# Hymba layer in float32: a scheduler that knows the shared port and measured steps, and small matmuls in runs of one array form

## Chip, cores and metric

One core of one Trainium2 chip. The metric is the device time of one launch in microseconds. PE is TensorE, PEld its weight loads, DVE is VectorE, ACT is ScalarE, POOL is GpSimd, SP is SyncE, which issues the DMAs. "Us" stands for microseconds throughout.

## The reference

One layer for 1024 prompt tokens and 8 samples of 4 tokens (1056 columns in all), in float32, model width 1024:

```python
def layer_forward(x, lw, rel_table, kv_cache, ssm_h0):
    h = rmsnorm(x, lw['norm_mix'])
    proj = h @ lw['w_in']                                    # 1024 -> q 512 | k 128 | v 128 | u 512
    q, k, v, u = jnp.split(proj, ...)                        # 8 query heads, 2 key heads of 64
    o_attn = band_attention(...)                             # blocks of 128 queries, window 128, bias, sinks
    o_ssm, h_last = s5_mixer(u, ssm_h0, ...)                 # 32 groups of 16 channels, state 64, then half-GLU
    merged = jnp.concatenate([rmsnorm(o_attn, ...), rmsnorm(o_ssm, ...)], axis=-1)
    x = x + merged @ lw['w_out']
    hm = rmsnorm(x, lw['norm_mlp'])
    x = x + jnp.square(jax.nn.relu(hm @ lw['w_up'])) @ lw['w_down']   # 1024 -> 4096 -> 1024
    return x, new_k, new_v, jnp.real(h_last), jnp.imag(h_last)
# afterwards: rmsnorm with norm_final
def s5_mixer(u, h0, ...):
    lam_bar = jnp.exp(lam * step)
    bu = jnp.einsum('blgc,gpc->blgp', u, b_bar)              # + lam_bar * h0 at the first token
    _, h = lax.associative_scan(combine, (a, bu), axis=1)    # h[t] = lam_bar h[t-1] + bu[t]
    y = jnp.real(jnp.einsum('blgp,gcp->blgc', h, c)) + d * u
    g = jax.nn.gelu(y)
    return g * jax.nn.sigmoid(g @ w_glu + b_glu), h[:, -1]
```

## The kernel before

Activations lie with channels on the partitions and tokens along the free axis, in rows of 128x1056. A large matmul (called bulk here) multiplies a 128x128 weight tile with a third of a row, 128x352. Each float32 operand is split into a high part, rounded for the fast float32 form of PE, and the rest; three products (high x high, low x high, high x low) accumulate in PSUM. 5760 bulk matmuls make up the in-projection, w_out, w_glu and the MLP. A weight piece of four tiles (`wr`, 256 KB) is split into `wh` (ACT or DVE) and `wl` (DVE or POOL), each with two buffers; `R` are 35 row buffers, `big` larger ones that live long, `PS` the eight PSUM banks. The program runs through: the split of x by rows and the first norm's sums; the in-projection; S5 in four steps s0 to s3 of eight groups each (tables by `F`, `K`; `X = F^T U` and its scan; `YT`); attention for the samples and for eight blocks b0 to b7; w_out; GELU and GLU; the SSM norm; the MLP; the last norm.

Small matmuls stand in between. `X` and `use` have 128 rows and 64 columns, in two column halves. In `att_block` a score matmul multiplies 64 rows (one key head, a half of the array's rows) by 128 columns, out 128x256: four query heads x three products for one key head, then a masked copy by DVE in PSUM, then the same for the other head in the other buffer of two banks (`pq2`). `PV` has 128 rows and 64 columns, out 64x512, one key head in each column half. The samples' PV has for each sample and head a matmul of 128 rows and one of 4 rows.

Nothing is issued in the order of the text. Every call is recorded as an `Op` (`Plan.record`) with a cost from `op_cost` for each engine that may do it (`ew` operations: DVE or POOL; copies: ACT or DVE). `Plan.schedule` then places one operation after another: of each engine the candidate that can start soonest, and among those with the same start the one with the highest priority, by the longest chain of costs behind it. Small matmuls get 100 on top there:

```python
                if e == "PE":
                    t = a[2][0].tile
                    p = group[t.mate] + (8.0 if t.units else 0.0) + (0.0 if o.bulk else 100.0)
...
                if cand is None or s < cand[0] - 1e-9 or (s <= cand[0] + 1e-9 and (p, -o.i) > cand[1]):
                    cand = (s, (p, -o.i), o, a)
```

`SCRIPT` gives the order of record and `BOOST` numbers for a few parts. `issue` emits the calls in the planned order, all from one line (L339), so groups in the profile are told apart by tiles and shapes. On the chip each engine runs its own list in order and waits for semaphores.

Of the kernel before, what the change touches and what calls it, by code (L numbers as in the profile page):

```python
# [18 lines left out]
# ---------------------------------------------------------------- planning: the kernel is written in program order, its  # L19
# operations are recorded, and a list scheduler puts them in the order in which they are issued  # L20
# [17 lines left out]
class View:  # L38
    """part of a planned tile: the elements it covers, and how the real tile gives it"""
# [33 lines left out]
class Op:  # L73
    __slots__ = ("alts", "tiles", "succ", "ndep", "prio", "avail", "i", "table", "src", "why", "s", "boost", "bulk")


QW = 0.5
# [4 lines left out]
TABLE = {AF.Exp: 1, AF.Tanh: 1, AF.Sin: 2, AF.Sqrt: 3}  # L82


def op_cost(eng, method, args, kw):
    out = args[0]
# [18 lines left out]
    if eng == "DVE":  # L105
# [8 lines left out]
        return (0.13 if psum and method == "scalar_tensor_tensor" else 0.07) + n / 960  # L114
# [4 lines left out]
    bc = len(vs) < 3 or any(a.ix.strides[-1] == 0 for a in vs[1:])  # L119
    return 0.15 + n * (1.66 if bc else 2.1) / 1000  # L120


class Plan:
# [4 lines left out]
    # -- tiles  # L128
# [11 lines left out]
    # -- operations  # L140
# [3 lines left out]
    def record(self, calls):  # L144
        o = Op()
        o.i, o.boost, o.bulk = len(self.ops), self.boost, self.bulk
        o.alts = [(e, m, a, k, op_cost(e, m, a, k)) for e, m, a, k in calls]
        a, k = calls[0][2:]
        views = [(v, True) for v in (a[0], k.get("accum_out")) if isinstance(v, View)]
        views += [(v, False) for v in (*a[1:], *(x for n, x in k.items() if n != "accum_out")) if isinstance(v, View)]  # L150
        o.tiles = list({v.tile: None for v, _ in views})
# [19 lines left out]
        if calls[0][0] == "PE":  # L171
            # accumulation groups of a bank stay in order
            v = a[0]
            key = v.box()[2] // 512
            prev = v.tile.last.get(key)
            if prev is not None and o.i not in prev.succ:
                prev.succ[o.i] = False
                o.ndep += 1
            v.tile.last[key] = o
# [7 lines left out]
    # -- the list scheduler  # L187
    def schedule(self):
# [5 lines left out]
        # a group of matmuls counts as its most urgent one  # L194
# [7 lines left out]
        table = [0]  # L202
        pend = {e: [] for e in ENG}
# [24 lines left out]
        def slot(t):  # L228
            """(time, units) of the best free place, or None"""
# [22 lines left out]
        while len(seq) < len(ops):  # L252
            best = None
            for e, lst in pend.items():
                cand = None
                fe = free[e]
                for o, a in lst:
                    s = max(fe, o.avail)
                    if cand is not None and s > cand[0] + 1e-9:
                        continue  # L260
                    if len(o.alts) > 1:
                        fin = s + a[4]
                        if any(b[0] != e and max(free[b[0]], o.avail) + b[4] + queue(b[0], o) < fin for b in o.alts):
# [38 lines left out]
            else:  # L302
# [4 lines left out]
                end = free[e] = s + c  # L307
            for t in o.tiles:
# [22 lines left out]
    # -- issue  # L331
    def issue(self, engines, make):
        res = lambda x: x.get() if isinstance(x, View) else x
        for n, (s, o, a) in enumerate(self.seq):
# [4 lines left out]
            getattr(engines[e], m)(*[res(x) for x in args], **{k: res(x) for k, x in kw.items()})  # L339
# [25 lines left out]
# rows: which ones a part of the kernel takes  # L365
# [6 lines left out]
# order of record up to the MLP  # L372
# [5 lines left out]
def body(tc, I, O, dbg=None):  # L378
# [6 lines left out]

    def dump(name, ap):
# [6 lines left out]
    def copy(out, in_):  # L393
        """ScalarE or VectorE"""
# [1073 lines left out]
```

## Time and profile before

| | us |
|---|---|
| time, median of 3 runs | 1217.54 |
| lowest, highest | 1208.55, 1219.12 |
| profiled execution, span from first to last instruction | 1209.6 |
| of it up to the start of the MLP (bulk matmul 1440) | 443.5 |
| mean granted clock of PE, share of full speed | 0.966 |

The profiled execution has no time of its own beside the span. The span is near the lowest of the three runs; sums below are made in it. PE's granted clock is a share of 2.4 GHz.

### The profile page before, as it was taken

How to read it: one execution, taken by the hardware profiler on the slowest of the kernel's cores; microseconds unless marked ns; L12 is line 12 of the kernel's file. 1: busy time of each engine (PE TensorE's matmuls, PEld its weight loads, DVE VectorE, ACT ScalarE, POOL GpSimd, SP SyncE). 2: the span in 40 equal slices, each digit the busy share in tenths (PEclk: the TensorE clock that was granted, in tenths of full speed). 3: DMA queues.
4: the chain of work that ended last, by engine and by line, in shares of the span. 5: the costliest groups of instructions: out<-in, count | busy, mean ns of one | idle time of the engine just before them, and what ended most of it. 6: DMA issues, size and time to landing. Idle time of an engine off the chain costs nothing.

```text
span 1209.6 us, 17482 instructions
## 1 busy us (share of the span) xinstructions
PE 1153.0 (95%) x7231; PEld 1109.0 (92%) x7231; DVE 670.9 (55%) x970; ACT 274.2 (23%) x512; POOL 277.0 (23%) x259
## 2 busy tenths in 40 slices
PE   6989999979888999999999999999999999999997
PEld 6888996658778999999999999999999999999996
DVE  8687747898789894522522533432432432534575
ACT  4212134632143321211111111111111111111241
POOL 4066414575463140020010010010011011000011
PEclk9989989969889999999999999999999999999997
DMA  6312320023331111111211111111111211121212
GB/s 234 102 47 71 98 46 11 9 47 93 85 99 44 37 44 43 44 44 44 53 44 45 53 44 36 52 44 44 53 44 45 53 44 44 44 52 44 79 54 92
DMA packets 55711, 69.71 MB, mean 58 GB/s; under 512 B 12184, under 2 KB 31808, under 8 KB 55616
## 3 DMA queue, kind: packets, MB, share of 16 engines
q1 hardware_dynamic: 55632, 68.59, 20.3%
q8 instruction: 57, 0.93, 0.4%
q14 instruction: 22, 0.18, 0.0%
HBM read 58.96 MB, written 6.15 MB: 54 GB/s over the span
## 4 chain that ended last, share of the span: by engine, by line
PE 69%; DVE 3%; ACT 1%; issue 0%; DVEq 0%; ACTq 0%; POOL 0%
PE PS L339 69%; DVE R L339 2%; DVE big L339 1%; ACT P L339 1%; ACT wh L339 0%; ACT R L339 0%; DVE wl L339 0%; DVE rsc L339 0%; DVE wh L339 0%; DVEq L1464 0%; ACT rsc L339 0%; ACTq L339 0%; DVE rs L339 0%; POOL R L339 0%; DVEq L339 0%
## 5 line engine op out<-in xcount | busy, mean ns | idle before, releaser
L339 PE MATMUL PS<-R,wh 128*128 128x352 f32 x3840 | 749.2, 326 | 19.4 <-DVE wh L339 10.1
L339 PEld LDWEIGHTS PS<-R,wh 128*128 128x128 f32 x3840 | 643.2, 191 | 25.6 <-DVE wh L339 10.5
L339 PE MATMUL PS<-R,wl 128*128 128x352 f32 x1920 | 430.1, 326 | 0.9 <-POOL wl L339 0.5
L339 PEld LDWEIGHTS PS<-R,wl 128*128 128x128 f32 x1920 | 331.5, 191 | 4.8 <-issue 2.1
L339 POOL TENSOR_TENSOR wl<-wr,wh 128x512 fp32r<-128x512 f32 x64 | 92.7, 1449 | 700.2 <-ACT wh L339 490.0
L339 ACT ACTIVATE wh<-wr 128x512 fp32r<-128x512 f32 x144 | 91.0, 632 | 649.9 <-PE PS L339 637.4
L339 DVE TENSOR_TENSOR wl<-wr,wh 128x512 fp32r<-128x512 f32 x96 | 70.2, 731 | 255.4 <-ACT wh L339 249.9
L339 DVE TENSOR_TENSOR big<-PS,big 128x1056 f32<-128x1056 f32 (+2 forms) x80 | 82.5, 1035 | 167.0 <-PE PS L339 166.9
L339 PE MATMUL PS<-R,R 128*128 128x384 f32 (+9 forms) x816 | 140.8, 342 | 19.1 <-DVE R L339 8.4
L339 PEld LDWEIGHTS PS<-R,R 128*128 128x128 f32 (+3 forms) x816 | 111.3, 196 | 40.2 <-POOL R L339 15.4
L339 DVE TENSOR_TENSOR R<-R,R 64x508 f32<-64x508 f32 (+8 forms) x55 | 44.6, 823 | 4.9 <-ACT R L339 4.3
L339 POOL TENSOR_TENSOR R<-R,R 128x512 f32<-128x512 f32 (+6 forms) x34 | 39.3, 1163 | 32.6 <-DVE R L339 23.9
L339 DVE TENSOR_TENSOR P<-P 128x1056 f32<-128x1056 f32 x32 | 40.3, 1259 | 6.6 <-ACT P L339 6.6
L339 DVE TENSOR_TENSOR P<-P,R 128x1056 f32<-128x1056 f32 x32 | 40.4, 1263 | 0.9
L339 DVE TENSOR_TENSOR R<-P,R 128x1056 fp32r<-128x1056 f32 x32 | 40.3, 1258 | 1.1
L339 ACT ACTIVATE R<-PS 128x512 f32<-128x512 f32 (+3 forms) x40 | 22.6, 570 | 75.9 <-PE PS L339 70.0
L339 ACT ACTIVATE P<-PS 128x1056 f32<-128x1056 f32 (+2 forms) x35 | 34.6, 988 | 8.8 <-PE PS L339 8.8
L339 ACT ACTIVATE R<-R 128x352 f32<-128x352 f32 (+4 forms) x32 | 25.8, 823 | 38.8 <-DVE R L339 38.5
L339 DVE SCALAR_TENSOR_TENSOR R<-R,R 128x352 f32<-128x352 f32 (+5 forms) x28 | 32.2, 1186 | 1.3 <-ACT R L339 1.3
L339 ACT ACTIVATE R<-R,sx 128x129 f32<-128x129 f32 x68 | 26.5, 392 | 22.7 <-DVE sx L339 22.7
L339 ACT ACTIVATE P<-big 128x384 f32<-128x384 f32 (+2 forms) x29 | 19.1, 662 | 50.5 <-DVE big L339 46.1
L339 POOL TENSOR_TENSOR big<-big,R 128x1056 f32<-128x1056 f32 x7 | 25.8, 3680 | 10.1 <-DVE big L339 9.9
(140 smaller groups left out, 691.1 us busy)
## 6 DMA issues: line engine op xcount, KB each, us to landing
wr<-in_w_up_dram SPq DMA_DIRECT2D x64, 256.0 KB
wr<-in_w_down_dram SPq DMA_DIRECT2D x64, 256.0 KB
R<-in_xT_dram SPq DMA_DIRECT2D x15, 528.0 KB
wr<-in_w_in_dram SPq DMA_DIRECT2D x20, 256.0 KB
wr<-in_w_out_dram SPq DMA_DIRECT2D x16, 256.0 KB
out_y_dram<-big SPq DMA_DIRECT2D x8, 384.0 KB
R<-R SPq DMA_DIRECT2D x32, 68.0 KB
R<-R SPq DMA_DIRECT2D x32, 64.0 KB
```

The lines of the kernel that those rows point to most:

```text
L339: getattr(engines[e], m)(*[res(x) for x in args], **{k: res(x) for k, x in kw.items()})
```

## The change

Five edits in the planner and in how small matmuls are recorded; `SCRIPT`, `BOOST` and the arithmetic stay, and comments are stripped.

- `op_cost` has other numbers for PE, DVE (operands with a stride of eight elements or more count 1.87 times) and POOL.
- `port` tells which DVE and POOL operations use the port that both share; such an operation isn't planned to start while one on the other engine is planned to run (`held`).
- `SWITCH`: a matmul whose array form (rows and columns of its weight tile, in classes 32, 64, 128) differs from that of the one before it is planned 0.2 later.
- `Run` records a group of small matmuls as one operation that nothing can come between: sums and rows of the norms, K, X, use, YT, transposes in fours, sample scores, PV.
- In `att_block` one run of 24 score matmuls alternates between the two key heads, into four banks at once (`pq4`); the four PV matmuls are a run; the samples' PV is done in two passes, all 128-row matmuls first and then all 4-row ones. A `start` flag then stands on the first matmul of a pass alone.

```diff
@@ op_cost
         if args[1].dt == F32R:
-            return 0.0025 + max(n, 256) / 2400
+            return max(0.056, 0.0133 + n / 2400)
         if m <= 64:
-            return max(0.06, 0.03 + n / 1200)
-        return max(0.134, 0.0025 + n / 600)
+            return max(0.107, n / 600)
+        return max(0.224, 0.013 + n / 600)
...
-        return (0.13 if psum and method == "scalar_tensor_tensor" else 0.07) + n / 960
+        slow = 1.87 if any(far(a) for a in vs) else 1.0
+        return (0.13 if psum and method == "scalar_tensor_tensor" else 0.07) + n / 960 * slow
...
-    bc = len(vs) < 3 or any(a.ix.strides[-1] == 0 for a in vs[1:])
-    return 0.15 + n * (1.66 if bc else 2.1) / 1000
+    return 0.16 + n * 1.75 / 1000
...
+def port(eng, method, args):
+    if method == "memset" or eng not in ("DVE", "POOL"):
+        return False
+    if eng == "POOL":
+        return True
+    big = [a for a in args[1:] if isinstance(a, View) and a.ix.size > a.ix.shape[0]]
+    sb = [a for a in big if a.tile.space != "PS"]
+    if method in ("tensor_scalar", "tensor_copy"):
+        return len(sb) == len(big) and args[0].tile.space != "PS"
+    return len(sb) > 1 or method == "tensor_tensor_scan"
@@ schedule
                     s = max(fe, o.avail)
+                    if e in o.port:
+                        s = max(s, held[other[e]])
+                    if e == "PE" and o.form != shape[0]:
+                        s += SWITCH
@@ class Run
+    def __exit__(self, *_):
+        c = self.calls
+        cost = sum(op_cost("PE", m, a, k) for m, a, k in c) / self.side
+        self.plan.record([("PE", *c[0])], c, cost)
@@ rs_sum
-            for b in blocks:
-                n = min(128, NT - b * 128)
-                c = (b - b0) * 128
-                pe.matmul(p[0:n, b - p0:b - p0 + 1], ss[:, c:c + n], ones_k, start=start, stop=stop)
+            for bs in ([b for b in blocks if b < 8], [b for b in blocks if b == 8]):
+                if bs:
+                    with run() as r:
+                        for b in bs:
...
+                            r.matmul(p[0:n, b - p0:b - p0 + 1], ss[:, c:c + n], ones_k, start=start, stop=stop)
@@ samples' PV
-            for b in range(8):
...
-                    pe.matmul(o, cvv[:, b, hp], PTc[:, u, c0:c0 + 16], start=True, stop=False)
-                    pe.matmul(o, vs4[:, b, hp], PTn[0:4, u, c0:c0 + 16], start=False, stop=True)
+            for part in range(2):
+                with run(2) as w:
+                    for b in range(8):
...
+                            if part == 0:
+                                w.matmul(o, cvv[:, b, hp], PTc[:, u, c0:c0 + 16], start=b == 0, stop=False)
+                            else:
+                                w.matmul(o, vs4[:, b, hp], PTn[0:4, u, c0:c0 + 16], start=False, stop=b == 7)
@@ att_block
+            pq_ = pq4()
+            with run(2) as u:
+                for j in range(4):
+                    for a, x, f, l in ((qh, kh, True, False), (qh, klr, False, False), (ql, kh, False, True)):
+                        for v in range(2):
+                            hp = half[v]
+                            o = pq_[:, 2 * v + j // 2, (j % 2) * 256 + 256 - n:(j % 2) * 256 + 256]
+                            u.matmul(o, a[hp, j], x[hp, kw], start=f, stop=l)
             for v in range(2):
-                hp = half[v]
-                pq = pq2()
-                for j in range(4):
-                    o = pq[:, j // 2, (j % 2) * 256 + 256 - n:(j % 2) * 256 + 256]
-                    pe.matmul(o, qh[hp, j], kh[hp, kw], start=True, stop=False)
-                    pe.matmul(o, qh[hp, j], klr[hp, kw], start=False, stop=False)
-                    pe.matmul(o, ql[hp, j], kh[hp, kw], start=False, stop=True)
```

What the planner makes of it, at three places. The numbers behind the names are the buffers' in the plan; a row names the output, the inputs, the output's shape and how often it stands there.

DVE in the split of x, before (each x row takes a TENSOR_SCALAR, `x times gain`, on DVE or ACT and a SCALAR_TENSOR_TENSOR, the rest; R_164 sums squares):

```order
L339 TENSOR_SCALAR R_169<-R_117,prm 128x1056
L339 SCALAR_TENSOR_TENSOR R_177<-R_117,prm,R_169 128x1056
L339 TENSOR_SCALAR R_188<-R_125,prm 128x1056
L339 SCALAR_TENSOR_TENSOR R_198<-R_125,prm,R_188 128x1056
L339 TENSOR_TENSOR R_164<-R_164,R_117 128x1056
L339 SCALAR_TENSOR_TENSOR R_222<-R_127,prm,R_202 128x1056
L339 SCALAR_TENSOR_TENSOR R_235<-R_131,prm,R_224 128x1056
L339 SCALAR_TENSOR_TENSOR R_249<-R_139,prm,R_237 128x1056
```

and now:

```order
L382 TENSOR_SCALAR R_168<-R_117,prm 128x1056
L382 SCALAR_TENSOR_TENSOR R_176<-R_117,prm,R_168 128x1056
L382 SCALAR_TENSOR_TENSOR R_193<-R_125,prm,R_183 128x1056
L382 SCALAR_TENSOR_TENSOR R_212<-R_128,prm,R_195 128x1056
L382 SCALAR_TENSOR_TENSOR R_231<-R_130,prm,R_214 128x1056
L382 SCALAR_TENSOR_TENSOR R_249<-R_135,prm,R_233 128x1056
L382 TENSOR_TENSOR wl_271<-wr_156,wh_258 128x512
L382 TENSOR_TENSOR wl_277<-wr_162,wh_263 128x512
L382 SCALAR_TENSOR_TENSOR R_286<-R_141,prm,R_251 128x1056
L382 SCALAR_TENSOR_TENSOR R_305<-R_147,prm,R_292 128x1056
L382 TENSOR_TENSOR R_149<-R_149,R_117 128x1056
```

The adds into the sum of squares (R_164, now R_149) left POOL, which had three of them among its first operations, and stand behind the splits on DVE.

PE at X of s0 (64x128, on `big`) and use (64x8), before:

```order
L339 MATMUL PS<-ident,R_832 128x128 x4
L339 MATMUL PS<-R_262,wl_778 128x352 x3
L339 MATMUL PS<-R_289,wh_757 128x352 x2
L339 MATMUL PS<-R_836,big_82 64x128 x16
L339 MATMUL PS<-R_289,wh_757 128x352
L339 MATMUL PS<-R_309,wh_757 128x352 x3
L339 MATMUL PS<-use_105,big_82 64x8 x16
L339 MATMUL PS<-R_289,wl_778 128x352 x3
L339 MATMUL PS<-R_119,wh_828 128x352 x3
```

and now, where bulk matmul 576 is the last ahead of it:

```order
L382 MATMUL PS<-R_305,wh_1025 128x352 x3
L382 MATMUL PS<-R_292,wl_1033 128x352 x3
L382 MATMUL PS<-R_841,big_82 64x128 x16
L382 MATMUL PS<-use_105,big_82 64x8 x16
L382 MATMUL PS<-R_1231,R_1250 128x32 x8
L382 MATMUL PS<-ident,R_1250 128x128 x8
L382 MATMUL PS<-ident,R_1030 128x128
L382 MATMUL PS<-ident,ks 32x128
```

X, use, the K and transposes of s1 moved from between the bulk matmuls of the in-projection to behind all of them. On DVE the rows ahead of the first operation on that X (TENSOR_TENSOR on PS and big) were, before:

```order
L339 TENSOR_TENSOR big_82<-t_6_894,t_7_896 64x4x128
L339 TENSOR_TENSOR Dd_297<-PS,Dd_297 128x128
L339 TENSOR_TENSOR big_82<-t_6_894,t_7_896 64x4x128
L339 TENSOR_TENSOR t_6_894<-L,R_490 128x512
L339 TENSOR_TENSOR R_933<-PS,big_82 128x512
L339 TENSOR_TENSOR R_939<-PS,big_82 128x512 x2
```

and now:

```order
L382 TENSOR_TENSOR wl_989<-wr_884,wh_983 128x512
L382 TENSOR_TENSOR R_1030<-PS,R_488 128x1056
L382 TENSOR_SCALAR ks<-R_1030 128x32
L382 TENSOR_TENSOR R_1054<-R_1030,R_1042 128x1056
L382 TENSOR_TENSOR wl_1080<-wr_996,wh_1074 128x512
L382 TENSOR_TENSOR wl_1126<-wr_1046,wh_1120 128x512
L382 TENSOR_TENSOR wl_1173<-wr_1087,wh_1166 128x512
L382 TENSOR_TENSOR wl_1213<-wr_1133,wh_1201 128x512
L382 TENSOR_TENSOR R_1225<-PS,big_82 128x512
L382 TENSOR_TENSOR R_1229<-PS,big_82 128x512 x2
```

Four weight splits (wl) and an evacuation of k (R_1030 from PS) came in front of it.

PE at the scores of block b1 (128x256) and the PV of b0 (64x512), before:

```order
L339 MATMUL PS<-R_1182,R_1776 128x256
L339 MATMUL PS<-R_1165,R_1776 128x256 x2
L339 MATMUL PS<-R_1182,R_1776 128x256
L339 MATMUL PS<-R_1165,R_1776 128x256
L339 MATMUL PS<-R_1807,R_1199 64x512
L339 MATMUL PS<-R_188,wl_1726 128x352
L339 MATMUL PS<-R_202,wh_1718 128x352
L339 MATMUL PS<-R_1165,R_1812 128x256
L339 MATMUL PS<-R_1182,R_1812 128x256
L339 MATMUL PS<-R_1165,R_1812 128x256 x2
L339 MATMUL PS<-R_1182,R_1812 128x256
L339 MATMUL PS<-R_1165,R_1812 128x256 x2
```

and now:

```order
L382 MATMUL PS<-R_1042,R_1805 128x256 x2
L382 MATMUL PS<-R_1054,R_1805 128x256 x2
L382 MATMUL PS<-R_1042,R_1805 128x256 x4
L382 MATMUL PS<-R_1054,R_1805 128x256 x2
L382 MATMUL PS<-R_1042,R_1805 128x256 x4
L382 MATMUL PS<-R_1054,R_1805 128x256 x2
L382 MATMUL PS<-R_1042,R_1805 128x256 x4
L382 MATMUL PS<-R_1054,R_1805 128x256 x2
L382 MATMUL PS<-R_1042,R_1805 128x256 x2
L382 MATMUL PS<-R_1871,R_1348 64x512
L382 MATMUL PS<-R_1873,R_1348 64x512
```

The scores of one head were twelve in a piece, with a PV matmul and bulk ahead of the other head's; now all 24 stand together, and both PV matmuls of b0 behind them.

## Rows read from the trace of the kernel before

**Rows 1.** page, part 1: busy us, share of the span, instructions

```profile
PE 1153.0 (95%) x7231; PEld 1109.0 (92%) x7231; DVE 670.9 (55%) x970; ACT 274.2 (23%) x512; POOL 277.0 (23%) x259
```

**Rows 2.** windows: length, busy us (instructions) of each engine, granted clock, DMA

```profile
0.00:443.50 443.50, 396.12 (x2511) 355.39 (x2512) 355.38 (x600) 147.43 (x320) 196.76 (x203) 0.93 0.27 72
443.50:1143.00 699.50, 699.16 (x4356) 696.87 (x4356) 274.17 (x279) 104.55 (x149) 70.83 (x48) 1.00 0.17 47
...
162.60:254.20 91.60, 88.78 (x493) 64.89 (x492) 71.37 (x128) 43.80 (x157) 43.70 (x38) 0.89 0.09 22
254.20:332.30 78.10, 63.61 (x419) 55.41 (x420) 67.45 (x99) 19.08 (x44) 41.77 (x43) 0.87 0.29 72
```

**Rows 3.** waits of PE, 0 to 443 us: total us, times, longest

```profile
PE PS L339 <- POOL R L339: 13.2, 7, 6.0
PE PS L339 <- DVE R L339: 12.1, 8, 4.5
PE PS L339 <- DVE wh L339: 10.1, 2, 5.7
```

**Rows 4.** waits of DVE, 0 to 443 us

```profile
DVE R L339 <- PE PS L339: 17.8, 7, 4.1
...
DVE wh L339 <- PE PS L339: 13.5, 4, 6.9
DVE PS L339 <- PE PS L339: 10.2, 9, 3.9
```

**Rows 5.** timeline of DVE, 11 to 32 us: start, us, operation [idle before]

```profile
12.19 1.32 DVE L339 SCALAR_TENSOR_TENSOR R<-R,prm,R 128x1056 fp32r<-128x1056 f32 x1
...
14.60 7.04 DVE L339 SCALAR_TENSOR_TENSOR R<-R,prm,R 128x1056 fp32r<-128x1056 f32 x3
...
28.96 1.25 DVE L339 TENSOR_TENSOR R<-R 128x1056 f32<-128x1056 f32 x1
```

**Rows 6.** timeline of POOL, 11 to 34 us

```profile
14.83 3.41 POOL L339 TENSOR_TENSOR R<-R,R 128x1056 f32<-128x1056 f32 x1 [13.61 <-DVE R L339]
```

**Rows 7.** timeline of DVE, 270 to 300 us

```profile
271.14 1.75 DVE L339 TENSOR_TENSOR R<-t,t 128x512 f32<-128x512 f32 x1
272.82 0.68 DVE L339 TENSOR_TENSOR R<-R 128x512 f32<-128x512 f32 x1
```

**Rows 8.** timeline of POOL, 270 to 300 us

```profile
270.64 1.71 POOL L339 TENSOR_TENSOR R<-R,cst 128x512 f32<-128x512 f32 x1
274.46 0.91 POOL L339 TENSOR_SCALAR R<-R 64x64 f32<-64x64 f32 x2 [2.12 <-DVE R L339]
```

**Rows 9.** timeline of PE, 120 to 300 us

```profile
121.11 2.02 PE L339 MATMUL PS<-R,R 128*64 128x128 f32 x32
...
124.36 1.10 PE L339 MATMUL PS<-use,R 128*64 128x8 f32 x32 [0.39 <-DVE R L339]
...
171.82 8.48 PE L339 MATMUL PS<-R,big 4*64 4x16 f32 x62
```

**Rows 10.** groups of PE by form, 162 to 258 us: busy us, mean ns

```profile
L339 PE MATMUL PS<-R,R 64*128 64x256 f32 x168 | 24.7, 311 | 2.1 <-DVE R L339 2.1
L339 PE MATMUL PS<-R,R 128*64 128x512 f32 x50 | 23.0, 636 | 0.7 <-ACT R L339 0.5 <-POOL R L339 0.2
```

**Rows 11.** groups of PE by form, 198.95 to 201 us

```profile
L339 PE MATMUL PS<-R,R 128*64 128x512 f32 x4 | 1.1, 618 | 0.0
```

**Rows 12.** groups of PE by form, 227.2 to 233 us

```profile
L339 PE MATMUL PS<-R,R 64*128 64x256 f32 x24 | 2.5, 295 | 0.0
```

**Rows 13.** timeline of DVE, 312 to 336 us

```profile
332.30 0.43 DVE L339 CAST wh<-wr 128x512 fp32r<-128x512 f32 x1 [6.90 <-PE PS L339]
```

More of the change, by code (lines that the diff above doesn't have):

```diff
@@ L73 @@
 class Op:
-    __slots__ = ("alts", "tiles", "succ", "ndep", "prio", "avail", "i", "table", "src", "why", "s", "boost", "bulk")
-QW = 0.5
+    __slots__ = ("alts", "tiles", "succ", "ndep", "prio", "avail", "i", "table", "src", "why", "s", "boost", "bulk", "port", "form", "run")
+QW, SWITCH = 0.5, 0.2
 ENG = ("PE", "ACT", "DVE", "POOL", "SP")
@@ L82, with far, form @@
 TABLE = {AF.Exp: 1, AF.Tanh: 1, AF.Sin: 2, AF.Sqrt: 3}
+def far(v):
+    st = [abs(b) for n, b in zip(v.ix.shape, v.ix.strides) if n > 1]
+    return bool(st) and st[-1] >= 8 * v.ix.itemsize
+def form(args):
+    up = lambda n: 32 if n <= 32 else 64 if n <= 64 else 128
+    return up(args[1].ix.shape[0]), up(args[1].ix.shape[-1])
 def op_cost(eng, method, args, kw):
@@ L142, in engine, with record @@
         return _Engine(self, names)
-    def record(self, calls):
+    def record(self, calls, run=None, cost=None):
         o = Op()
+        o.run = run
         o.i, o.boost, o.bulk = len(self.ops), self.boost, self.bulk
-        o.alts = [(e, m, a, k, op_cost(e, m, a, k)) for e, m, a, k in calls]
+        o.alts = [(e, m, a, k, cost or op_cost(e, m, a, k)) for e, m, a, k in calls]
+        o.port = {c[0] for c in calls if port(c[0], c[1], c[2])}
+        o.form = form(calls[0][2]) if calls[0][0] == "PE" else None
         a, k = calls[0][2:]
@@ L171, in record @@
         if calls[0][0] == "PE":
[L173 to L179, printed above, removed]
+            for v in [a[0]] + [r[1][0] for r in (run or [])[1:]]:
+                key = v.box()[2] // 512
+                prev = v.tile.last.get(key)
+                if prev is not None and prev is not o and o.i not in prev.succ:
+                    prev.succ[o.i] = False
+                    o.ndep += 1
+                v.tile.last[key] = o
         for t in o.tiles:
@@ L202, in schedule @@
         table = [0]
+        held = {"DVE": 0.0, "POOL": 0.0}
+        other = {"DVE": "POOL", "POOL": "DVE"}
+        shape = [None]
         pend = {e: [] for e in ENG}
@@ L262, in schedule @@
                         fin = s + a[4]
-                        if any(b[0] != e and max(free[b[0]], o.avail) + b[4] + queue(b[0], o) < fin for b in o.alts):
+                        if any(b[0] != e and max(free[b[0]], o.avail, held[other[b[0]]] if b[0] in o.port else 0.0) + b[4]
+                               + queue(b[0], o) < fin for b in o.alts):
                             continue
@@ L307, in schedule @@
                 end = free[e] = s + c
+                if e in o.port:
+                    held[e] = end
+                if e == "PE":
+                    shape[0] = o.form
             for t in o.tiles:
@@ L384, in body, with run @@
     ett, ets = ew.tensor_tensor, ew.tensor_scalar
+    def run(side=1):
+        return Run(plan, side)
     def dump(name, ap):
@@ L866, in s5 @@
             p = ps1()
-            for r in range(2):
-                for a in range(4):
-                    for h in range(2):
-                        hp = half[h]
-                        c0 = r * 32 + a * 8
-                        pe.matmul(p[hp, c0:c0 + 8], Fv[:, r, a, hp], use[:, 2 * a + h], start=True, stop=True)
+            with run(2) as u:
+                for r in range(2):
+                    for a in range(4):
+                        for h in range(2):
+                            hp = half[h]
+                            c0 = r * 32 + a * 8
+                            u.matmul(p[hp, c0:c0 + 8], Fv[:, r, a, hp], use[:, 2 * a + h], start=True, stop=True)
             hw = new("hw")
@@ L1035, in probs @@
             p = pt1()
[L1036 to L1037 removed]
+            with run() as u:
+                for j in range(4):
+                    u.transpose(p[:, j * 128:(j + 1) * 128], S[:, j, 0:128], ident)
             PT = row(R_T)
```

116 lines of the change are left out of this document (68 added, 48 removed).

## The prediction, made before the result

> **What bounds the kernel now.** The page's sums first: PE is busy 95% of the span, DVE 55%, POOL 23% [rows 1]. The windows by stage then show two kernels in one. From 443.5 us on, PE has no gap at full clock (699.16 of 699.50 us, 4356 matmuls, 0.160 us each) [rows 2]; nothing in the change reaches the rate of that part, so it keeps its 766 us to the end. What can move is the 443.5 us ahead of it, where PE is busy 396.1 us and its clock averages 0.93 [rows 2]: some 47 us of gaps, and a slow clock on part of the rest. I cut it where the order has steps: rstd ready (46.0), first masked score of attention (162.6), last (254.2), end of S5 (332.3), first MLP matmul (443.5).
>
> The waits say who is late. PE waits for POOL 13.2 us, for DVE's rows 12.1, for DVE's weight split 10.1 [rows 3]; DVE waits for PE 17.8, 13.5 and 10.2 us [rows 4]. So it is a relay in which each stands still for the other, and a shorter step pays only while its engine is the late one.
>
> One thing makes DVE late. Its 128x1056 split step takes 1.32 us at 12.19, and three of them from 14.60 take 7.04, 2.35 each, while POOL's add of the same width runs 3.41 [rows 5, 6]. Its 128x512 operation takes 1.75 us beside POOL's 1.71 and 0.68 when POOL has stopped [rows 7, 8]. Summed over its rows before the MLP, DVE's durations come to about 390 us, and to 331 if each form took its shortest time: some 60 us of stretch.
>
> **Part 1, costs and the shared port.** The new costs and the port rule make POOL unattractive: by the order POOL's instructions fall from 264 to 176, DVE's rise from 972 to 1040, ACT's from 446 to 466. Each row at the shortest duration of its form, DVE's work before the MLP rises from 331 to 360 us (+29) and POOL's falls from 234 to 171 (-63). The stretch must shrink: in proportion to POOL's work it would be 60 x 171/234 = 44 us, and none if the plan kept the two wholly apart. DVE's net is thus +29-16 = +13 to +29-60 = -31. I take -15, near the middle, because the plan's starts drift from real ones. The clearest piece is the x split, where POOL's adds now stand behind DVE's splits: the five stretched steps return to 1.32, and one 1.25 us add [rows 5] comes back to DVE: -5 us on the way to the first full stream of matmuls. In the MLP DVE is busy 274 and ACT 105 of 699.5 us [rows 2]; what moves between them there is hidden behind PE.
>
> The Trainium skill ("SBUF — State Buffer", Who interferes with whom) calls this an exclusive lock: a VectorE instruction with two SBUF inputs and a GpSimd one that reads SBUF don't share, the later waits for the whole of the earlier. Rows 7 and 8 agree (1.75 against 0.68 + part of 1.71). By that rule alone the two engines' work adds up, and the change takes 63-29 = 34 us from what they share; rival 1 comes near that by another way.
>
> **Part 2, runs of one form on PE.** Priced where rows show both forms.
> - Sample PV: 62 matmuls that alternate 128-row and 4-row forms take 8.48 us; 32 of one form take 1.10 [rows 9]. Two passes of 32: 2.2. Saves 6.
> - PV of the blocks: 50 records, 25 matmuls, 23.0 us, 0.92 each [rows 10]. A pair that happens to stand side by side on the two column halves takes 1.1, 0.55 each [rows 11]. All 30 in runs: 30 x 0.37 = 11 us; I take 10.
> - Scores: 168 in 24.7 us, 0.147 each [rows 10]; a run of 24 in one stretch takes 2.5, 0.104 each [rows 12]. Now the key heads alternate between the row halves. No row shows row halves alternating. The bounds: 0 if they queue, and 168 x (0.147-0.052) = 16 if they overlap wholly at the hot price. The nearest row is the column halves: 32 matmuls that alternate take 2.02 us, 0.063 each [rows 9], which is overlap. I take 13.
> - The 4-matmul transposes, K, use and YT runs: order rows say these mostly stood together before; 0 to 2 us, I take 1.
>
> Together 30 us of PE. But they lie in the stage from 162.6 to 254.2, where PE's 88.8 us busy stand beside DVE's 71.4 [rows 2], and DVE waits 10.2 us there for the scores [rows 4]. With PE faster DVE ends last: its work there is 67 us by summed shortest durations against 65, plus stretch that remains (about 7) and the wait for the first scores of each block, now a run of 24 for both heads instead of 12. I get 81 to 85 us instead of 91.6, -8. PE's 30 us are thus worth 8; the rest turns into PE gaps.
>
> **Part 3, the switch penalty moves the order.** 0.2 us on a start in another form makes any ready bulk matmul precede any small one, whatever its priority. The order shows it: X of s0 (on big, 64x128) stood behind bulk matmul 353 and now behind 576, the last of the in-projection, with use, K, X of s1, YT of both and the sample scores bunched behind it. DVE issues in order; in front of its X step now stand four weight splits, each of which needs a buffer that 36 bulk matmuls free. 36 x 0.160 = 5.8 us a piece [rows 2], 23 us for work of some 4: a hole of about 18 us in DVE, from about 105 to 126. It isn't all loss, since those bulk matmuls run then without gaps (bulk 576 at about 125), and they no longer fill PE inside attention (24 bulk rows there instead of 74). But DVE's chain S5 to attention starts late. Likewise the last 32x1 sum of the first norm moves from bulk 144 to 216, and the evacuations behind it stand after 29 parameter steps of DVE: +5 to +6 us, which eats the -5 of the x split. Nothing hides it: PE's banks are full there.
>
> **The sum**, on the profiled execution (its span is 1209.6, close to the lowest of the runs, 8 under their median): start, -5+5.5 = 0; hole 18, less 3 of stretch saved and 5 of small steps that now run back to back: first masked score +10 (173); attention -8, so its last at about +3 (257); then DVE loses its 6.9 us wait for PE [rows 13], 4 us of POOL waits go [rows 3], and 2 us of stretch, so S5 and GLU end 10 ahead of where +3 would put them: -7. Bulk matmuls left behind the SSM norm are 236 instead of 284 (7.7 us less): between -3 and -10 more, of which most is hidden behind DVE, I take -3. MLP begins 10 us earlier, at about 433, and runs as before. 1217.5-10 = 1208.
>
> **Rivals.**
> 1. *Stretch relief carries all the way* (faster). The hole is filled by what DVE has ready, because real weight loads come sooner than I walk them, so first masked score at 163; attention -8 to -10; S5 -10. -27 in all: 1190. For it: the 60 us of stretch are real and 88 instructions leave POOL. Against: DVE's order is fixed, and no independent step stands between its four splits.
> 2. *Starved S5* (slower). One mechanism: small matmuls behind all bulk. The hole is 23 us and the parameters' delay 6, and, the filler being spent, PE in attention falls to its lower clock as it did with fewer matmuls: in 254.2 to 332.3 the clock is 0.87 at 63.6 of 78.1 us busy [rows 2]. Then scores and PV cost half of what they save, attention gives back only 3, and the tail 6: +29-5-3-6 = +15, 1232. It decides as soon as X of s0 comes after about 130 us.
> 3. *Row halves don't overlap* (no change). 24 scores stay at 2.5 to 4 us and DVE waits for both heads: 7 blocks x 1.2 us back: 1216.
> 4. *It doesn't do what it says.* The port is held apart in the plan only; the real stretch stays in proportion, DVE +13 instead of -15. A third of that lies on the path: about +9, so 1217.
>
> The Trainium skill ("TensorEngine Tiling (Array Packing)", Key Properties) says that a change of tiling mode drains the engine and that tiles run in parallel; the first agrees with 8.48 against 1.10 us [rows 9]. By the second rival 3 would fall; no run here shows it for row halves.
>
> **Chances.** A measurement of this kernel tells about 1% from no change (the runs spread over 0.9%). Forecast, 1200 to 1215: 0.40. Rival 1: 0.27. Rival 2: 0.17. Rival 3: 0.10. Rival 4: 0.06. Faster by over 1% (under 1205.4) are rival 1 nearly whole and two fifths of the forecast: 0.42. Slower by over 1% (over 1229.7) are rival 2 and a little of 4: 0.19. Within 1%: 0.39. The range runs from rival 1's 1190, less 4 for the sure end of the scores, to rival 2's lower half: 1186 to 1230; both signs hold much, and the forecast's own is 1200 to 1215.
>
> **What would show it.** Runs of 24 scores near 1.5 us (overlap) or over 2.5 (rival 3); sample PV near 2.3; a PV run of 4 near 2.1; DVE's 128x512 operations nearer 0.68 than 1.2 on the mean; a DVE gap of some 18 us ahead of X of s0; PE waiting for DVE soon after bulk 216; first masked score near 173 and MLP near 433. Wrong I am if that gap is filled (then rival 1) or if the bulk matmuls left for behind attention wait for DVE all the same (then 2).

## The result, and the profile after

The changed kernel takes 1257.2 us in the median of 4 runs (1255.9 to 1263.4), the kernel before 1214.2 in four; the ratio of the two is put at 1.037, 95% interval 1.0316 to 1.0423. It is slower by 3.7%, outside the range of 1186 to 1230. The profiled execution spans 1254.4 us against 1209.6, so 44.8 us have to be found.

The page's first part, as [rows 1]:

```profile
PE 1138.1 (91%) x7231; PEld 1100.1 (88%) x7231; DVE 650.1 (52%) x1038; ACT 297.1 (24%) x532; POOL 174.4 (14%) x171
```

PE's share fell from 95% to 91%, and that of POOL from 23% to 14%. DVE has less busy time than before, 650.1 against 670.9 us, though it issues more: most of the stretch is gone, and the kernel is slower all the same.

Windows by stage of the kernel after, to be read against [rows 2]: from bulk matmul 216 to 576, from there to the first masked score of attention (191.8), to the last (281.4), to the end of S5 (363.9), to the first MLP matmul (481.1), to the last bulk matmul. Columns as there, PE, PEld, DVE, ACT, POOL, clock:

```profile
47.30:127.90 80.60, 71.11 (x426) 67.01 (x426) 49.72 (x190) 16.67 (x26) 8.85 (x23) 0.94 0.25 70
127.90:191.80 63.90, 37.81 (x368) 34.86 (x367) 44.11 (x102) 10.78 (x27) 15.65 (x18) 0.79 0.28 63
191.80:281.40 89.60, 66.15 (x484) 49.22 (x486) 72.01 (x131) 42.72 (x150) 38.96 (x39) 0.83 0.11 25
281.40:363.90 82.50, 64.33 (x424) 57.09 (x421) 62.71 (x119) 17.73 (x41) 14.66 (x16) 0.83 0.28 75
363.90:481.10 117.20, 102.62 (x582) 99.25 (x582) 88.98 (x99) 45.15 (x61) 26.07 (x11) 0.88 0.17 46
481.10:1189.00 707.90, 701.18 (x4358) 699.21 (x4357) 265.39 (x267) 122.53 (x166) 65.69 (x50) 0.99 0.16 47
```

| stage | before | after | change |
|---|---|---|---|
| start to first masked score | 162.6 | 191.8 | +29.2 |
| attention | 91.6 | 89.6 | -2.0 |
| from there to the MLP | 189.3 | 199.7 | +10.4 |
| MLP's bulk matmuls | 699.5 | 707.9 | +8.4 |
| tail | 66.6 | 65.4 | -1.2 |

In the 63.9 us ahead of attention PE is busy 37.8 and runs at 0.79 of full clock.

The samples' PV and the first runs of scores are as short as they were meant to be; timeline of PE in attention:

```profile
202.81 2.15 PE L382 MATMUL PS<-R,big 128*64 128x16 f32 x64
...
211.66 2.71 PE L382 MATMUL PS<-R,R 64*128 64x256 f32 x28
215.48 0.35 PE L382 MATMUL PS<-R,R 64*128 64x256 f32 x1 [1.12 <-DVE R L382]
216.05 1.69 PE L382 MATMUL PS<-R,R 64*128 64x256 f32 x23 [0.22 <-DVE R L382]
```

Yet in attention PE's busy time fell from 88.8 to 66.2 us, 22.6 less, and the stage is 2 us shorter: PE's gain became PE's gaps. The waits of PE up to 490 us, against [rows 3]:

```profile
PE PS L382 <- DVE R L382: 52.7, 18, 10.4
PE PS L382 <- DMA R<-R: 11.3, 2, 10.0
PE PS L382 <- POOL R L382: 9.6, 5, 4.6
```

52.7 us for DVE instead of 12.1, and 11.3 for a DMA that isn't among [rows 3].

Where it starts is seen in the timeline of DVE (the bracket is idle time and its releaser):

```profile
104.97 1.26 DVE L382 TENSOR_TENSOR R<-PS,R 128x1056 f32<-128x1056 f32 x1 [4.88 <-PE PS L382]
...
110.96 0.69 DVE L382 TENSOR_TENSOR wl<-wr,wh 128x512 fp32r<-128x512 f32 x1 [2.32 <-ACT wh L382]
117.32 0.69 DVE L382 TENSOR_TENSOR wl<-wr,wh 128x512 fp32r<-128x512 f32 x1 [5.67 <-ACT wh L382]
123.75 0.69 DVE L382 TENSOR_TENSOR wl<-wr,wh 128x512 fp32r<-128x512 f32 x1 [5.73 <-ACT wh L382]
128.28 0.69 DVE L382 TENSOR_TENSOR wl<-wr,wh 128x512 fp32r<-128x512 f32 x1 [3.84 <-ACT wh L382]
```

These are the four weight splits ahead of X of s0, each waiting for the rounded half that waits for bulk matmuls: 17.6 us of idle DVE, 22.4 with the wait at 104.97. PE comes to X of s0 at 127.94, with bulk 576 behind it, and then walks through the bunch. The first line is X of s0 in the kernel before, the last the load that YT of s1 waits for:

```profile
92.08 2.44 PE L339 MATMUL PS<-R,big 128*64 128x128 f32 x32
...
127.94 1.97 PE L382 MATMUL PS<-R,big 128*64 128x128 f32 x32
...
141.96 3.60 PE L382 MATMUL PS<-R,R 128*128 128x32 f32 x16 [10.43 <-DVE R L382]
...
154.93 1.10 PE L382 MATMUL PS<-use,R 128*64 128x8 f32 x32 [2.07 <-DVE R L382]
...
175.62 6.49 PE L382 MATMUL PS<-R,R 128*128 128x136 f32 x32 [9.95 <-DMA R<-R]
...
171.63 0.43 SPq L382 DMA_DIRECT2D R<-kd  x1
```

K of s1 waits 10.43 us for DVE, which from 129 to 142 us works on X and the scan of s0 and on the tables of s1. YT of s1 waits 9.95 us for a DMA. U isn't it, though the bracket says R<-R: U's pieces were issued from 143.1 to 150.9 and had landed by 152.8. It is the table that K of s1 makes, which goes to DRAM (`kd`) and comes back: its load is issued only at 171.63, behind the samples' small loads in SP's list, its last packet lands at 175.48, and PE goes on at 175.62. In 127.9 to 182 PE has only small matmuls to issue, each at the end of a chain through DVE, while the next bulk matmul stands behind all of them in its list. Then 48 bulk matmuls (577 to 624) stand ahead of the first scores, and DVE waits for ACT (7.20 us) and for PE (5.31):

```profile
185.54 0.18 DVE L382 RECIPROCAL sx<-sx 128x4 f32<-128x4 f32 x1 [7.20 <-ACT R L382]
...
191.75 1.41 DVE L382 SCALAR_TENSOR_TENSOR R<-PS,rs,R 128x512 f32<-128x512 f32 x2 [5.31 <-PE PS L382]
```

The bunch itself isn't what got dearer. From the start of X of s0 to the first masked score the kernel before takes 70.5 us (92.08 to 162.61) and the changed one 63.8 (127.94 to 191.75). The 29.2 us are 35.9 by which X of s0 starts later, less 6.7. Before, some 240 bulk matmuls (354 to 593) ran inside those 70.5 us; now 48 do, and PE has gaps instead.

### The profile page after: what moved, and what is told of

It is laid out like the page before. It is cut to its first block, busy times and chain, and to the rows that moved or that the text cites. A ratio compares the mean times of both kernels' runs of the same rounds, so it can differ in the third digit from the quotient of the medians.

```text
span 1254.4 us, 17423 instructions
## 1 busy us (share of the span) xinstructions
PE 1138.1 (91%) x7231; PEld 1100.1 (88%) x7231; DVE 650.1 (52%) x1038; ACT 297.1 (24%) x532; POOL 174.4 (14%) x171
## 4 chain that ended last, share of the span: by engine, by line
PE 81%; DVE 13%; ACT 2%; issue 2%; SPq 1%; DMA 1%; POOL 0%; DVEq 0%; ACTq 0%; POOLq 0%
PE PS L382 81%; DVE R L382 8%; DVE big L382 2%; DVE P L382 1%; SPq L382 1%; ACT R L382 1%; DVE wl L382 1%; DVE t L382 1%; ACT wh L382 0%; DVE PS L382 0%; ACT L382 0%; DVE sx L382 0%; POOL R L382 0%; DMA R<-R 0%; DVE rsc L382 0%
## 5 line engine op out<-in xcount | busy, mean ns | idle before, releaser
L382 DVE TENSOR_TENSOR wl<-wr,wh 128x512 fp32r<-128x512 f32 x102 | 75.3, 739 | 298.2 <-ACT wh L382 297.9
L382 POOL TENSOR_TENSOR wl<-wr,wh 128x512 fp32r<-128x512 f32 x58 | 77.7, 1340 | 695.9 <-ACT wh L382 625.8
L382 PE MATMUL PS<-R,R 128*128 128x384 f32 (+9 forms) x816 | 130.1, 363 | 48.6 <-DVE R L382 33.0
L382 PEld LDWEIGHTS PS<-R,R 128*128 128x128 f32 (+3 forms) x816 | 105.7, 210 | 68.6 <-POOL R L382 27.2
L382 ACT ACTIVATE R<-PS 128x512 f32<-128x512 f32 (+4 forms) x42 | 23.2, 561 | 106.8 <-PE PS L382 81.1
L382 DVE TENSOR_TENSOR R<-R,R 128x512 f32<-128x512 f32 (+8 forms) x71 | 46.6, 676 | 1.3 <-ACT R L382 0.8
L382 PE MATMUL PS<-ident,R 128*128 128x128 f32 x110 | 20.9, 328 | 13.2 <-DVE R L382 8.6
L382 PEld LDWEIGHTS PS<-ident,R 128*128 128x128 f32 x110 | 14.9, 170 | 19.6 <-issue 9.5
L382 POOL TENSOR_TENSOR P<-P,P 128x1056 f32<-128x1056 f32 (+1 forms) x7 | 16.4, 2341 | 102.5 <-ACT P L382 102.5
```

## Experiments

Theory S: the penalty takes the precedence of small matmuls away, so S5 and attention start late. Rival P: the port rule and new costs overload DVE. Rival R: the runs hold attention up. The ratio is to the kernel before, on the same chip, with its 95% interval.

| run | edit, against the changed kernel unless said | us | ratio (interval) |
|---|---|---|---|
| e1 | no penalty | 1206.3 | 0.993 (0.991 to 0.996) |
| e2 | no port rule | 1286.4 | 1.060 (1.055 to 1.064) |
| e3 | runs alone | 1221.4 | 1.006 (1.004 to 1.009) |
| e4 | no penalty, no port rule | 1229.6 | 1.012 (1.008 to 1.016) |
| e5 | penalty 0.01 | 1266.6 | 1.042 (1.037 to 1.047) |
| e6 | penalty one way | 1200.4 | 0.988 (0.983 to 0.993) |
| e7 | e1 without runs | 1209.0 | 0.995 (0.992 to 0.997) |
| e8 | e1, head after head | 1215.2 | 0.999 (0.996 to 1.002) |
| e9 | kernel before, with the penalty | 1295.2 | 1.067 (1.063 to 1.071) |
| e10 | 32-wide forms spared | 1255.4 | 1.034 (1.030 to 1.038) |
| e11 | e1, no POOL | 1206.1 | 0.992 (0.989 to 0.995) |
| e12 | e1, old costs | 1188.3 | 0.980 (0.975 to 0.985) |
| e13 | e1, old PE costs | 1207.4 | 0.995 (0.993 to 0.998) |
| e14 | e1, old DVE and POOL costs | 1189.4 | 0.981 (0.977 to 0.984) |
| e15 | e12, penalty one way | 1186.5 | 0.978 (0.975 to 0.982) |

### Which part does it: e1 to e4

```diff
-QW, SWITCH = 0.5, 0.2
+QW, SWITCH = 0.5, 0.0          # e1, e3, e4
...
 def port(eng, method, args):
-    if method == "memset" or eng not in ("DVE", "POOL"):
-        return False
+    return False                # e2, e3, e4; e3 has op_cost of the kernel before as well
```

> The changed kernel with the switch penalty at 0 in place of 0.2; runs, port and costs stay. By the order X of s0 then stands behind bulk matmul 390 instead of 576 and X of s1 behind 507. Theory S (the penalty starves the S5 matmuls behind bulk, so S5 and attention start late): the first attention score comes before 170 us instead of 190, the PE gaps ahead of the MLP fall from about 100 us to under 65, and the time falls by 25 to 45 us, to 1212 to 1232. Rival P (the port rule and the new costs put too much on DVE): POOL has even fewer instructions here (157 against 176), so the time stays at 1245 to 1265. Rival R (the runs themselves, 24 scores into four banks, hold attention up): stays within 10 us of 1257.

> The changed kernel without the port rule (no operation counts as using the shared port); penalty, runs and costs stay. POOL gets 292 instructions instead of 176, X of s0 stays behind bulk matmul 576. Theory S: the late start stays, and the stretch of DVE comes back on top, so 1250 to 1275. Rival P: DVE is relieved, 1215 to 1235. Rival R: 1250 to 1265.

> The kernel before with the runs alone: penalty 0, no port rule, the old costs. X of s0 stands behind bulk matmul 356, POOL has 252 instructions. Theory S: the gain on the small matmuls is there without the starvation, so 1195 to 1220, same or faster than before. Rival P: likewise 1195 to 1220. Rival R: 1240 to 1260, since the runs are what is left of the change.

> Runs and the new costs, without penalty and port rule: POOL has 293 instructions, X of s0 stands behind bulk matmul 345. Theory S: 1195 to 1225. Rival P: 1195 to 1225 too, and faster than the kernel that keeps the port rule and drops the penalty, by 20 us or more. If the port rule helps as planned, it is the other way round: this one is slower than that by 5 to 15 us. Rival R: 1240 to 1260.

Without the penalty 51 us go, more than the 43 that the whole change cost, and the first score comes at 163.5 instead of 190.2 us. The time is under the expected 1212 to 1232; the place is the expected one. By the stages of the table above e1 takes 165.1, 93.8, 180.9, 698.9 and 66.9 us: the penalty costs 26.7 us up to the first masked score, 18.8 between attention and the MLP and 9.0 in the MLP, and in attention the kernel with it is 4.2 faster. In all seventeen kernels of this document the first masked score follows the start of X of s0 by 64 to 77 us (66.5 in e1), so the place of X of s0 sets the start of attention.

Taking the port rule away makes it worse, by 29 us with the penalty (e2, above the expected 1250 to 1275) and by 23 without (e4 against e1; 5 to 15 were expected, and e4 lies above the 1195 to 1225 of theory S), so rival P's port is the wrong way round; its costs come back below. The kernel with the runs alone is 0.6% slower than the one before: not rival R's 1240 and more, and no gain either, just over the 1195 to 1220 of theory S. What the port rule does is read from one DVE operation, groups by form up to 400 us, in e4 without the rule and in e1 with it, against 1239 ns in the kernel before:

```profile
L381 DVE TENSOR_TENSOR t<-L,R 128x512 f32<-128x512 f32 x12 | 14.8, 1234 | 0.1
```

```profile
L382 DVE TENSOR_TENSOR t<-L,R 128x512 f32<-128x512 f32 x20 | 14.5, 760 | 0.1
```

### Size or order of the penalty: e5, e6, e9

```diff
-QW, SWITCH = 0.5, 0.2
+QW, SWITCH = 0.5, 0.01                                                          # e5
...
-                    if e == "PE" and o.form != shape[0]:
+                    if e == "PE" and o.form != shape[0] and shape[0] != (128, 128):   # e6
```

e9 adds to the kernel before the function `form`, the field `shape` and these two lines of the change with 0.2:

```diff
+                    if e == "PE" and o.form != shape[0]:
+                        s += 0.2
```

> The changed kernel with a penalty of 0.01 us instead of 0.2. Two theories of how the penalty does harm. Theory O (order): the planner picks by earliest start, so any positive penalty takes the precedence of small matmuls away; by the order X of s0 again stands behind bulk matmul 576; time 1245 to 1268, as with 0.2. Theory Z (size): 0.2 us is dearer than a switch is, a twentieth of it would do little: 1203 to 1215, as with no penalty.

> The penalty of 0.2 kept, but charged only where the matmul before was a small form, never where a small one follows bulk. X of s0 then stands behind bulk matmul 392. Theory O: only the direction bulk before small does harm, so 1200 to 1212, like the kernel without penalty. If instead any penalty spoils the plan (the order of small forms among themselves counts as well): 1225 or more.

> The kernel before with the switch penalty alone: no runs, no port rule, old costs. By the order X of s0 goes from bulk matmul 353 to 576 and X of s2 and s3 stay at 720 and 792; YT of s2 and s3 go from 804 to 854 to 972 to 975. Theory O (the penalty by itself starves the small matmuls): 30 to 70 us slower than before, 1245 to 1285. If the penalty only hurts together with the other edits: within 12 us of before.

A twentieth of the penalty does as much harm (1266.6), the full one charged in the other direction does none (1200.4), and the penalty alone spoils the kernel before by 6.7%, ten us beyond what was expected of it. So it isn't the 0.2 us. The planner takes the candidate with the smallest start; PE is behind in the plan, so every candidate's start is the time at which PE gets free, and the 100 that small matmuls get in priority decides. Any positive amount on top of the start ends that tie before priority is asked.

### What 32-wide matmuls cost: e10

```diff
-                    if e == "PE" and o.form != shape[0]:
+                    if e == "PE" and o.form != shape[0] and o.form not in ((128, 32), (32, 128)):
```

> The changed kernel, penalty 0.2, but matmuls with a weight tile of 32 rows or 32 columns are spared it. X of s0 stays behind bulk 576 and YT of s3 even goes to 1008, so the late S5 stays. What changes are the last 32-token blocks of the norms: the first norm's last sum goes from bulk 216 back to 167, the MLP norm's last row matmul from 1800 back to 1494. Theory O for these: the gap of PE before bulk 217 shrinks by 5 us or more, and the wait of 6.4 us for ACT in the MLP goes, so the MLP's bulk matmuls (1440 to the last) take 699 to 701 us instead of 708. The time in all 1235 to 1262, depending on s3. If the MLP's loss comes from the casts moved to ACT, it stays at 706 or more.

The MLP's 8.4 us are the penalty's too. In the changed kernel's MLP one matmul of 32 tokens, the last of the norm's row, stands at bulk 1800 where it stood at 1499, by the order. Timelines of PE and of ACT there:

```profile
492.43 3.35 PE L382 MATMUL PS<-ident,rs 128*128 128x128 f32 x16
...
544.91 0.40 PE L382 MATMUL PS<-ident,rs 32*128 32x32 f32 x2
551.71 2.13 PE L382 MATMUL PS<-R,wh 128*128 128x352 f32 x6 [6.39 <-ACT P L382]
```

```profile
547.10 3.42 ACT L382 ACTIVATE R<-P 128x1056 fp32r<-128x1056 f32 x3 [1.55 <-DVE P L382]
550.60 2.22 ACT L382 ACTIVATE P<-PS 128x1056 f32<-128x1056 f32 x2
```

DVE's product of the square with the norm needs that row. Three buffers P are full by then; ACT does three casts in a row (3.42 us) before it frees the PSUM banks, and PE waits 6.39. With that matmul spared PE has no wait over 0.3 us in the MLP, and the window of its bulk matmuls has 698.6 us (the time in all hardly moves, 1255.4, since the MLP begins 4.3 us later there):

```profile
485.40:1184.00 698.60, 698.26 (x4356) 696.42 (x4355) 269.55 (x272) 117.31 (x161) 65.26 (x50) 1.00 0.17 47
```

In the start the expectation failed. The first norm's last sum is back at bulk 167, and bulk 288 ends at 78.9 us, at 79.1 in the changed kernel: that sum was covered.

### The runs and the heads: e7, e8

```diff
-        cost = sum(op_cost("PE", m, a, k) for m, a, k in c) / self.side
-        self.plan.record([("PE", *c[0])], c, cost)
+        for m, a, k in c:                                                        # e7
+            self.plan.record([("PE", m, a, k)], None, op_cost("PE", m, a, k) / self.side)
...
+            for v in range(2):                                                   # e8
                 for j in range(4):
                     for a, x, f, l in ((qh, kh, True, False), (qh, klr, False, False), (ql, kh, False, True)):
-                        for v in range(2):
```

> Without penalty, and the small matmuls recorded one by one instead of in runs (their order of record, the alternating heads, the four banks and the two passes stay, but others can come between). X of s0 stands behind bulk 390 as with runs. If the runs themselves gain what they save on PE: slower than the kernel without penalty by 8 to 20 us, 1214 to 1226. If PE isn't late there, as the sum of the prediction had it in attention: within 6 us of 1206.

> Without penalty, runs kept, but the 24 scores stand one key head after the other instead of alternating. The order of everything else is the same. If the two row halves overlap only when they alternate, a run of 24 takes 2.4 to 2.6 us instead of 1.7; by time that is at most 7 x 0.8 = 6 us: 1206 to 1212. If they overlap in any order or never: 1.7 us or no difference from the alternating run.

Loose matmuls cost nothing that can be told (intervals overlap), so no gain is shown for holding runs together. The order of the heads does count. Timelines of PE at the scores of b1, e1 (alternating) and e8:

```profile
177.38 1.69 PE L382 MATMUL PS<-R,R 64*128 64x256 f32 x24
```

```profile
179.19 2.75 PE L382 MATMUL PS<-R,R 64*128 64x256 f32 x24
```

0.070 us for a score against 0.115, both at a granted clock of 1.00. At the rate of the bulk matmuls (0.160 us for 352 columns, [rows 2]) 256 columns take 0.116, which is one score after the other; 0.070 is less than one alone would take. So the row halves overlap when neighbours in the list lie in different halves, and not when twelve of one half come first. Rival 3's doubt is settled: they overlap. The Trainium skill ("TensorEngine Tiling (Array Packing)", Key Properties) says that tiles operate independently; these two runs agree, and add that the order in the list decides whether there is anything to overlap. In time e8 is 9 us slower by the medians and 7 by the ratios, above the 6 expected. At full clock the eight runs of scores take 8.4 us longer (seven times 1.06, and 0.95 in b0), but attention only 4.2 (97.9 us against 93.8): half of it doesn't reach the time. By the spans, 8.0 us apart, the rest is 0.9 up to the first masked score, 1.2 ahead of the MLP and 1.6 behind it, and no cause is shown for that.

### POOL and the costs: e11 to e15

```diff
-    ew = plan.engine("DVE", "POOL")
+    ew = plan.engine("DVE")                                                      # e11
...
-            return max(0.056, 0.0133 + n / 2400)                                 # e12, e13, e15; the other two PE lines too
+            return 0.0025 + max(n, 256) / 2400
...
-        slow = 1.87 if any(far(a) for a in vs) else 1.0                          # e12, e14, e15
+        slow = 1.0
...
-    return 0.16 + n * 1.75 / 1000                                                # e12, e14, e15
+    bc = len(vs) < 3 or any(a.ix.strides[-1] == 0 for a in vs[1:])
+    return 0.15 + n * (1.66 if bc else 2.1) / 1000
```

> Without penalty, with the port rule, runs and new costs, and POOL taken out of the choice altogether: all its elementwise work goes to DVE (1200 instructions there, 10 on POOL). DVE then has no stretch at all, and some 60 us more work before the MLP than with POOL's 157. If the stretch is worth more than POOL's help: within 8 us of 1206 or faster. If POOL's share under the port rule is real relief: 1225 to 1260.

> Without penalty, with the port rule and the runs, but the costs of the kernel before. POOL has 144 instructions, X of s0 stands behind bulk 404. If the port rule alone makes the gain: 1200 to 1213, like the kernel with the new costs. If the measured costs are needed with it: 1218 or more.

> Without penalty, port rule and runs kept, new costs for DVE and POOL, old costs for PE. Theory CP (it is the dearer PE costs that spoil the plan): near 1188, as with all costs old; 1183 to 1197. Theory CE (it is the DVE and POOL costs): near 1206, 1200 to 1212. If neither of the two alone does it, in between.

> The mirror of the run before: new costs for PE, old ones for DVE and POOL. Theory CP: 1200 to 1212. Theory CE: 1183 to 1197.

> Port rule, runs, old costs, and the penalty charged only where the matmul before was a small form. With the new costs the one-way penalty was 6 us faster than none (1200 against 1206). If its gain is its own, it adds to the old costs': 1180 to 1188. If the two gains are the same one (plans that happen to fall well): 1186 to 1198.

Without POOL the time is the same as with it (1206.1, 1206.3). Under the port rule POOL is no relief: in attention DVE is busy 81.3 us without it instead of 74.0, and idle 11.9 instead of 19.8, in a stage of the same length (93.2 and 93.8). That the turns DVE waits in the plan eat the relief is argued from this, not shown. Up to the MLP DVE is busy 10.6 us longer, not the 60 that were expected. The new costs lose 18 us, and the mirror runs put all of it on those of DVE and POOL (e14 1189.4, e13 1207.4). Part of where: DVE's evacuation of the first results of the in-projection (8 operations of 128x352 from PSUM), which frees the banks for bulk 217 on. Timelines of DVE in e1, e12 and e14:

```profile
57.25 4.39 DVE L382 TENSOR_TENSOR R<-PS,R 128x352 f32<-128x352 f32 x8
```

```profile
51.84 4.39 DVE L382 TENSOR_TENSOR R<-PS,R 128x352 f32<-128x352 f32 x8
```

```profile
49.45 4.49 DVE L383 TENSOR_TENSOR R<-PS,R 128x352 f32<-128x352 f32 x8
```

It comes 5 to 8 us earlier with the old costs (62.4 us in the changed kernel), and bulk 288 ends at 76.5, 68.5 and 64.7 us. By stage e12 gains 8.5 us up to the first masked score (156.5 against 165.1) and 9.8 in attention (84.0 us against 93.8), and from there on under 1 us a stage; what it is in attention was not taken further. Expected of e12 were 1200 to 1213, so its 1188.3 was a surprise, which e13 and e14 were made for. The one-way penalty takes 2 us from e12, within both intervals and in the ranges of both forecasts: no separate gain shown. e12, e14 and e15 beat both kernels, by 2.0 to 2.2% against the one before; their intervals are clear of no change, but not of gains under 2%.

## Why the prediction was wrong

The mechanism of rival 2 happened, at 0.17, and its price was three times too small: 15 us written, 45 measured. Up to the end of attention rival 2 was near (+21 written, +27.2 measured); behind it, it wrote -6, and +17.6 came. Point by point:

- **The step that failed** is the price of part 3, the penalty. It is counted once, as "hole 18, less 3 of stretch saved and 5 of small steps that now run back to back: first masked score +10", and put at nothing behind attention and in the MLP. The hole of DVE was as computed, 17.6 us at the four splits, and the credits of 8 are near the 6.7 us by which the way from X of s0 to the first masked score got shorter. What was wrong is to take DVE's idle time for the delay. X of s0 starts 35.9 us later, and both numbers for that stood in the prediction: from behind bulk 353 to behind 576 are 223 matmuls at 0.160, 35.7 us. +29.2 instead of +10. With the other two places the penalty costs 49 us by the spans (the changed kernel against e1).
- Nor was the way behind X of s0 walked. It is a chain through DVE and a DMA that small matmuls can't shorten: 54 us from 127.9 to 182, with PE busy for 28 of them. The kernel before hid it behind bulk matmuls; the order now had spent them.
- I called bulk 576 the last of the in-projection, and had the small matmuls "behind all of them" ahead of that. It has 720; two of its ten channel blocks came after. Had I asked why these 144 matmuls weren't in the hole of PE after 128 us, the chain would have been seen: the order puts them behind the whole bunch.
- The x split: bulk 144 ends at 32.5 instead of 38.3 us, -5.8 for -5. Right. The first norm and evacuations: +5.5 were written; from bulk 144 to bulk 288 the changed kernel loses 13.6. The cause named second, the evacuation behind DVE's parameters, is the larger one: without the penalty the same stretch still loses 10.1, and with the old DVE and POOL costs next to nothing (43.1 us in e1, 34.9 in e12, 33.3 in e14, 33.0 before). The 32x1 sum is not (e10).
- PE's prices held at full clock: two passes of sample PV take 2.15 us at 202.81 (2.2 forecast), 24 alternating scores 1.69 (1.5). Over attention they didn't: its clock is 0.83 where it was 0.89, as rival 2 had it. Scores come to 0.098 us each and PV to 0.71, by these two groups of PE from 191.8 to 285 us against [rows 10]. Over 168 scores and 30 PV that saves 8 and 6 us, where 13 and 10 were written. PE's 22.6 us less also hold 31 bulk matmuls fewer (96 for 127), about 5 us, so they aren't near the 30.

```profile
L382 PE MATMUL PS<-R,R 128*64 128x512 f32 x52 | 18.5, 717 | 0.4 <-POOL R L382 0.4
L382 PE MATMUL PS<-R,R 64*128 64x256 f32 x168 | 16.4, 341 | 7.9 <-DVE R L382 5.0 <-ACT R L382 2.2 <-POOL R L382 0.6
```

- PE's saving is worth 2 us in attention instead of 8. DVE is busy 72.0 us (74 forecast), and still idle for 17.6 where 7 to 11 were left over: it is a relay, as the opening said, and the sum forgot it. It isn't the penalty's doing, since e1 takes 93.8 us there.
- The 8.48 us of the samples' PV, on which a saving of 6 rests, were read as the price of changing form alone. Five of them ran at half clock (the windows at the end of this document). That 6 was saved is thus in part luck.
- The stretch went as forecast, DVE's operation on R and R of 128x512 from 1185 to 774 ns, and e1 against e4 shows the port rule's worth, 23 us, in which the moves of work between the engines are contained. Rival 4 falls.
- From attention to the MLP: -13 written (from +3 to -10), +10.4 measured. Without the penalty it is -8.2 (180.9 us in e1), so the step was near and the penalty's 18.8 us were missing. By the order YT of s3 stands at bulk 894 instead of 854 and the SSM norm's sums at 1204 and 1224 instead of 1156 and 1171; which of them it is wasn't separated.
- "Nothing in the change reaches the rate of that part" was said of the MLP. One small matmul was enough for 8.4 us (e10).
- The new costs of DVE and POOL were priced only in the +5.5 at the start. They take 18 us (e1 against e12 and e14), half of it in attention.

Shown: the penalty by its order (e1, e5, e6, e9), the MLP (e10), the port rule (e2, e4), DVE and POOL costs (e13, e14). Only argued: which of the late matmuls costs the 18.8 us ahead of the MLP, why DVE still stands idle in attention, and where there the new costs lose 9.8.

## What to carry to other kernels

In a list scheduler that picks by earliest start, an amount added to the start isn't a price but a rank: where the engine is behind, any positive amount outweighs all priorities. Put such a cost where it can't reorder what is urgent (one way, or into the priority). Price a bunched-up group by how much later its first member starts, not by the gap that another engine shows, and walk the chain behind it to its end, DMA trips included, before crediting the engine's gaps as filled; a PE matmul that is cheaper is worth only what the engine that it feeds was waiting for.

## What the hardware showed unexpectedly

Row halves of the array overlap for neighbours in the list: 24 scores of 64 rows in 1.69 us alternating, 2.75 one half after the other. Matmuls of 128 and of 4 rows that alternate took 8.48 us for 62 [rows 9]; 64 in two passes took 2.15. A part of that is the clock, as two windows of the kernel before show (PE's busy time and matmuls first, the granted clock third from the end; the matmul that runs on an edge counts too):

```profile
171.82:175.00 3.18, 3.18 (x31) 2.80 (x30) 0.30 (x1) 0.00 (x0) 1.21 (x1) 1.00 0.31 82
175.10:180.30 5.20, 5.20 (x34) 4.60 (x33) 0.00 (x0) 0.00 (x0) 0.00 (x0) 0.50 0.00 0
```

At full clock that is about 0.11 us for a matmul, against 0.034 in the passes, also at full clock. How much of the 0.07 is the change of form, and how much that the two column halves no longer overlap, isn't separated here. And POOL's work was worth nothing beside DVE under the port rule: with 157 instructions on POOL or with 10 the time was the same (ratios 0.993 and 0.992).
